# Output projection and router of a transformer block: elementwise work from GpSimd to VectorE, the second norm's variance by ScalarE, two weight loads on another queue

## The chip, the core and the metric

The kernel runs on one core of one Trainium2 chip. A core has five engines that work side by side, each through its own instructions in order: TensorE (PE, matrix products and transposes), VectorE (DVE), ScalarE (ACT), GpSimd (POOL) and SyncE (SP, which here only issues DMA transfers). They meet through semaphores: an instruction that needs another engine's result waits, and everything behind it on its own engine waits too. The metric is device time in microseconds (us) for one execution; less is better.

## What is computed

The reference is one layer of a diffusion transformer on 1024 tokens of width 1024: two kinds of attention, an output projection, two layer norms, and a mixture of 16 experts in which each expert picks its 128 best tokens. The part that the change touches is this:

```python
mix = (sigmoid(g_mla) * (y_mla @ w_proj_mla) + sigmoid(g_na) * (y_na @ w_proj_na)) @ w_out
x_new = layer_norm(ALPHA * x + g1 * mix, ln1_g, ln1_b)
u2 = layer_norm(x_new) * (1 + sc2) + sh2
aff = softmax(u2 @ w_router)              # 16 experts
g, idx = top_k(aff.T, 128)                # each expert's tokens
xe = u2[idx]                              # gathered, then the experts' FFN
```

All of it is float32. The big products split each operand into a high and a low part (hi, lo) and run three products for one.

## The kernel before

The order of instructions on each engine is the order in which the Python code is written; no scheduler moves anything. After attention (which ends near 951 us of the profiled span) three stages follow, then the experts (from about 1213 us to the end).

**Mix stage**, 951 to 1056 us. `split(hi, lo, src, eng)` (L85) makes the two parts: ScalarE copies the high part, then `eng` subtracts it from the source to give the low part. The attention output `yT` is split in 16 pieces of 128x512; a list `POOL` gives five of these to GpSimd. A loop over `m` (8 blocks of 128 output columns) and `b` (two halves of the tokens) then runs 24 products each, and `gates()` (L1150 and following) on VectorE multiplies them by the stored sigmoid gates (`t`, L1153) and adds the two halves into `mix` (L1156). In each `m` SP loads the gates (`sg`, L1080), a block of `w_out` (`wos`, L1131) and the next block of projection weights (`raw`, L1007); the next gate load waits for a buffer that `gates()` frees. `wos_load` multiplies the `w_out` block by `g1b` on GpSimd (L1132). Eight blocks of 128x1024 of `wos` are then split for the output projection (`wo_split`), two of them (`WOP`) with their low part on GpSimd.

**Output and router stage**, 1056 to 1180 us: eight products `main(t, ps, between)`, one for each 128 tokens, each of two halves (b = 0, 1) of 24 matmuls (L1233). The dictionary `between` hangs other work in front of a given matmul group (b, kt). During product t the following runs:
- at its start `pre_mix(t + 1)` splits the next product's input: ScalarE's copy, then the low part on GpSimd (L87, 128x1024);
- `half(t, 0)` and, at the end, `half(t, 1)`: residual and statistics (L1243, L1244) on VectorE;
- `norms(t)` after it: first layer norm on VectorE, with the power -0.5 on GpSimd (L99, `lr`), then the statistics of the second norm (L1264, L1248), its own power on GpSimd, and `nm`, a 128x1 product (L1273);
- for the tokens of t - 1: `route` (transposes L1293 on PE, copied out by ScalarE as `uT`, L1294), `norms2` (L1280 on ScalarE, then L1281 and L1282 on GpSimd, 128x1024 each), `logits` (PE L1301, copied out as `part`), `softmax` (a PE product `collect` L1308, then L1321 to L1331 on VectorE with an Exp on ScalarE);
- `store(t - 2)`: two DMA issues on ScalarE's queue (L1253, L1254).

**Router's end**, 1180 to 1205 us: for expert 0 the rank of each token is counted by comparisons (`compare`, masks on VectorE and GpSimd; `count` on PE), `pick` (L1454) finds its tokens, and `fetch` (L1461) gathers their rows of u2 by an indirect DMA on GpSimd's queue. The first expert's products wait for this transfer.

**Expert weights** come in 1 MB tiles through a ring of 17 buffers (`slot_of_ring`, `load_next`, L1213), in the order in which the experts use them. The ring takes over the buffers of the stages before as these fall free: tiles 13 and 14 use the last `wo` pair.

Of the kernel before, what the change touches and what calls it, by code (L numbers as in the profile page):

```python
# [27 lines left out]
def block_kernel(ctx, tc, a, out, dbg=None):  # L28

    nc = tc.nc  # L30
# [971 lines left out]
    with ExitStack() as st:  # L1002
# [11 lines left out]
        nxt = [(hi, lo)]  # L1014
        POOL = ((0, 3), (1, 5), (1, 7), (1, 1), (1, 3))
# [98 lines left out]
        def pre_mix(t, pieces=1):  # L1114
# [4 lines left out]
            def piece(i):  # L1119
                ks = slice(i * w, (i + 1) * w)  # L1120
                split(hi[:, ks], lo[:, ks], m[:, ks], nc.gpsimd if t else nc.vector)
            return [lambda i=i: piece(i) for i in range(pieces)]

        def wo_split(b, g):
            hi, lo = wo[b, g] = big_tile(), big_tile()
            for k in range(0, 4, 2):
                split(hi[:, k:k + 2], lo[:, k:k + 2], wos[:, 4 * g + k:4 * g + k + 2, b * 512:(b + 1) * 512],
                      nc.gpsimd if (b, 2 * g + k // 2) in WOP else nc.vector)
# [5 lines left out]
        WOP = ((1, 0), (1, 3))  # L1134
        wos_load(0)
# [80 lines left out]
    with ExitStack() as st:  # L1216
# [18 lines left out]

        sts, mv2, u2s, nms = {}, {}, {}, {}

# [18 lines left out]
        def norms(t):  # L1256
            xt = xts[t]
            mv, r = aggregate(sts.pop(t))
            nc.vector.scalar_tensor_tensor(xt, xt, mv[:, 0:1], l1g, op0=OP.subtract, op1=OP.mult)
            for c in (H0, H1):  # L1260
                nc.vector.scalar_tensor_tensor(xt[:, c], xt[:, c], r[:, 0:1], l1b[:, c], op0=OP.mult, op1=OP.add)
            st = p.tile([128, 2, 6], F32, name="st2", bufs=2)
            for b, c in enumerate((H0, H1)):
                nc.vector.bn_stats(st[:, b], xt[:, c])  # L1264
            if t == 7:
                compare(5, 7, 0, 6, nc.gpsimd)
            mv, r = mv2[t] = aggregate(st)
            u2s[t] = p.tile([128, D], F32, name="u2", bufs=2)
            if t == 7:
                nc.vector.scalar_tensor_tensor(u2s[t][:, H1], xt[:, H1], mv[:, 0:1], sc2b[:, H1], op0=OP.subtract, op1=OP.mult)  # L1270
                nc.vector.scalar_tensor_tensor(u2s[t][:, H1], u2s[t][:, H1], r[:, 0:1], sh2b[:, H1], op0=OP.mult, op1=OP.add)
            nms[t] = p.tile([128, 1], F32, name="nm", bufs=2)
            nc.vector.scalar_tensor_tensor(nms[t], mv[:, 0:1], -1.0, r[:, 0:1], op0=OP.mult, op1=OP.mult)  # L1273

        def norms2(t):

            c = H0 if t == 7 else slice(0, D)
            u2, (mv, r) = u2s[t], mv2[t]
            nm = nms.pop(t)
# [107 lines left out]
        for t in range(8):  # L1387
# [9 lines left out]
            else:  # L1397
                between[0, 7] = lambda: route(t - 1, 0)
                between[1, 0] = lambda: route(t - 1, 1)
                between[1, 2] = lambda: (norms2(t - 1), logits(t - 1))  # L1400
                between[1, 4] = lambda: softmax(t - 1)
            if t >= 2:
                between[0, 3] = lambda: store(t - 2, nc.scalar)
            if t == 7:
# [3 lines left out]
                between[0, 1] = lambda: spread(0, 6)  # L1408
                between[0, 5] = between[0, 6] = load_next
                between[1, 3] = lambda: [compare(j, 6) for j in range(3)]  # L1410
# [12 lines left out]
        store(6, nc.scalar)  # L1423
        logits(7)
        compare(5, 7, 6, 7, nc.gpsimd)
        compare(6, 7, 0, 7, nc.gpsimd)
        collect(7)
        compare(3, 6)
        count(rank, 3)
        softmax0(7)  # L1430
        for _ in range(3):
            load_next()
        norms2(7)
        store(7, nc.sync)
        compare(4, 7)
        count(rank, 4)
        softmax1(7)
        spread(7, 8)
# [26 lines left out]
        fetch(xe0, idx0)  # L1465
        while pos[0] < RB - 2:
            load_next(nc.gpsimd)
        pt = ps_T()
# [458 lines left out]
```

## Time and profile before

| | us |
|---|---|
| median of 3 runs (lowest, highest) | 1846.52 (1845.69, 1850.57) |
| the profiled execution | 1849.55 |
| its span, first to last instruction | 1847.8 |
| busy in the span: PE, DVE, ACT, POOL | 1693.6, 1202.8, 939.4, 688.2 |
| eight products and router's end, 1056 to 1205 us | 149 |

The profile gives for each engine when it was busy and, for an idle stretch, whose signal ended it. A busy engine is not always at work: an instruction that is held up after its start counts as busy. Start times are us from the span's start. A row of the timeline merges like instructions (xN) and shows, in brackets, the idle time before it and what ended this.

### The profile page before, as it was taken

To read this page: it belongs to the slowest core of one execution; us is meant where nothing else is said; L and a number is where in the kernel's file an instruction comes from. 1 tells how busy PE (TensorE), PEld (TensorE's weight loads), DVE (VectorE), ACT (ScalarE), POOL (GpSimd) and SP (SyncE) were. 2 spreads that over 40 slices of the span, in tenths; PEclk is the share of its full clock that TensorE was granted. 3 is DMA by queue.
4 is the path that set the end of the run, shared out by engine and by line. 5 is a ranking of instruction groups with operands and counts; after the bars stand their busy time and mean duration, and the time that the engine had idled before them with its cause. 6 is when DMAs were issued, how large, how long until landed. Compare 5 with 4: busy or idle time off the path is not lost.

```text
span 1847.8 us, 25506 instructions
## 1 busy us (share of the span) xinstructions
PE 1693.6 (92%) x9633; PEld 1344.2 (73%) x9633; DVE 1202.8 (65%) x1849; ACT 939.4 (51%) x1479; POOL 688.2 (37%) x528
## 2 busy tenths in 40 slices
PE   5999998999899999999999888778999999999992
PEld 3778787888778877777767666446887887888872
DVE  5612242203477766655563588877999999999987
ACT  3422222111467766666650222244777777777765
POOL 1335455532244421221022355555434423533134
PEclk9999999999999999999999999879999999999996
DMA  8333645245344220110026443687999999999943
GB/s 319 110 108 146 227 167 176 94 118 158 82 87 87 54 54 20 28 30 2 1 88 202 151 182 143 233 314 267 347 396 369 391 391 366 388 391 379 374 158 124
DMA packets 96891, 356.63 MB, mean 193 GB/s; under 512 B 28368, under 2 KB 36944, under 8 KB 70912
## 3 DMA queue, kind: packets, MB, share of 16 engines
q1 hardware_dynamic: 77744, 283.68, 42.4%
q0 software_dynamic: 11664, 43.52, 7.7%
q10 hardware_dynamic: 7360, 27.81, 3.9%
q8 instruction: 75, 1.23, 0.3%
q14 instruction: 48, 0.39, 0.1%
HBM read 312.85 MB, written 42.12 MB: 192 GB/s over the span
## 4 chain that ended last, share of the span: by engine, by line
PE 66%; DVE 12%; DMA 7%; POOL 7%; issue 3%; ACT 3%; SPq 1%; ACTq 0%; POOLq 0%; DVEq 0%
PE pS L401 10%; PE pY L921 4%; DMA rawm<-in_w_mod_dram 4%; PE pT L894 4%; PE pgate L90 3%; PE pD L90 3%; PE pD L92 3%; PE pD L91 3%; PE pup L90 3%; PE pup L91 3%; PE pup L92 3%; PE pgate L92 3%; PE pgate L91 3%; DMA raw<-in_w_proj_dram 2%; PE pS L90 2%
## 5 line engine op out<-in xcount | busy, mean ns | idle before, releaser
L1690 DVE TENSOR_TENSOR hl<-raw,hl 128x1024 fp32r<-128x1024 f32 x183 | 221.7, 1238 | 23.0 <-ACT hl L1689 21.0
L1689 ACT ACTIVATE hl<-raw 128x1024 fp32r<-128x1024 f32 x188 | 194.0, 1056 | 40.4 <-PE pgate L92 19.4
L87 DVE TENSOR_TENSOR wlo<-raw,whi 128x1024 fp32r<-128x1024 f32 x25 | 37.6, 1508 | 148.6 <-ACT whi L86 148.5
L1589 POOL TENSOR_SCALAR oh<-iot,slot 128x128 bf16<-128x128 f32 x112 | 133.2, 1204 | 0.5
L401 PE MATMUL pS<-uhi,whi 128*128 128x512 f32 (+1 forms) x440 | 131.0, 386 | 2.3 <-DVE stg L488 1.5
L401 PE MATMUL pS<-ulo,whi 128*128 128x512 f32 (+1 forms) x440 | 129.0, 382 | 0.0
L401 PE MATMUL pS<-uhi,wlo 128*128 128x512 f32 (+1 forms) x440 | 128.6, 381 | 0.0
L306 POOL TENSOR_TENSOR sb<-qs,sa 128x512 fp32r<-128x512 f32 x28 | 35.9, 1283 | 240.5 <-DVE sa L305 110.0
L1793 POOL DMA_INDIRECT acc_d<-ye,idx x15 | 35.3, 2351 | 242.2 <-DVE ye L1788 242.2
L1689 ACT ACTIVATE whl<-raw 128x1024 fp32r<-128x1024 f32 x94 | 99.7, 1060 | 43.7 <-PE pgate L92 20.0
L1690 DVE TENSOR_TENSOR whl<-raw,whl 128x1024 fp32r<-128x1024 f32 x91 | 112.1, 1232 | 9.4 <-ACT whl L1689 8.5
L905 ACT ACTIVATE pt<-pT 128x512 f32<-128x512 f32 x128 | 69.7, 595 | 95.2 <-PE pT L894 95.0
L1690 DVE TENSOR_TENSOR raw<-raw 128x1024 fp32r<-128x1024 f32 x92 | 112.4, 1222 | 6.6 <-ACT raw L1689 6.6
L1689 ACT ACTIVATE raw<-raw 128x1024 fp32r<-128x1024 f32 x94 | 99.4, 1058 | 22.8 <-PE pD L92 8.2
L376 POOL TENSOR_TENSOR rawm<-rawm,scol 128x1024 f32<-128x1024 f32 x32 | 63.1, 1971 | 127.3 <-DMA rawm<-in_w_mod_dram 127.3
L880 DVE TENSOR_REDUCE sn<-pS 128x1 f32<-128x1024 f32 x64 | 78.3, 1223 | 40.5 <-PE pS L92 40.3
L1233 PE MATMUL pS<-raw,hl 128*128 128x512 f32 x384 | 97.8, 403 | 3.3 <-DVE t L1153 2.2
L401 PEld LDWEIGHTS pS<-uhi,whi 128*128 128x128 f32 x440 | 78.9, 188 | 22.9 <-issue 3.9
L894 PE MATMUL pT<-ident,pm 128*128 128x128 f32 x640 | 94.5, 278 | 1.2 <-ACT pt L905 1.0
L401 PEld LDWEIGHTS pS<-ulo,whi 128*128 128x128 f32 x440 | 80.2, 188 | 16.4
L921 PE MATMUL pY<-pt,v 128*64 128x256 f32 x640 | 82.5, 389 | 10.5 <-ACT inv L721 10.5
L401 PEld LDWEIGHTS pS<-uhi,wlo 128*128 128x128 f32 x440 | 80.1, 188 | 16.3
(482 smaller groups left out, 4773.4 us busy)
## 6 DMA issues: line engine op xcount, KB each, us to landing
raw<-in_w_exp_down_dram SPq DMA_DIRECT2D x64, 1024.0 KB
raw<-in_w_exp_gate_dram SPq DMA_DIRECT2D x63, 1024.0 KB
raw<-in_w_exp_up_dram SPq DMA_DIRECT2D x63, 1024.0 KB
rawm<-in_w_mod_dram POOLq DMA_DIRECT2D x32, 512.0 KB, 3.8
raw<-in_w_in_dram SPq DMA_DIRECT2D x25, 512.0 KB
wm<-in_w_mod_dram SPq DMA_DIRECT2D x8, 1024.0 KB
sig_d<-stg ACTq DMA_DIRECT2D x16, 512.0 KB
sg<-sig_d SPq DMA_DIRECT2D x32, 256.0 KB
```

The costliest lines, as they stand in the source:

```text
L90: nc.tensor.matmul(ps, ahi, bhi, start=first, stop=False)
L91: nc.tensor.matmul(ps, ahi, blo, start=False, stop=False)
L92: nc.tensor.matmul(ps, alo, bhi, start=False, stop=last)
L401: nc.tensor.matmul(pt[:, c0:c1], ww[:, kt], uu[:, kt, c0:c1], start=(kt == 0 and k == 0), stop=(kt == KT - 1 and k == 2))
L880: nc.vector.tensor_reduce(sm[:, 0:1], ps, axis=AX.X, op=OP.max)
L894: nc.tensor.transpose(tb[b][:, (k - k0) * 128:(k - k0 + 1) * 128], Pm[n][:, k * 128:(k + 1) * 128], ident)
L905: nc.scalar.activation(dst, src, AF.Copy)
L921: nc.tensor.matmul(py[0][h * 64:(h + 1) * 64, 0:256], vm[:, k, col:col + 64], PT[g, h][:, k], start=(k == 0), stop=(k == 9))
L1233: nc.tensor.matmul(ps[b], x[:, kt], w[:, kt % 4], start=(kt == 0 and k == 0), stop=(kt == 7 and k == 2))
L1589: nc.gpsimd.tensor_scalar(ohb[:, t], iot, slot[:, t, e:e + 1], None, op0=OP.is_equal)
L1689: nc.scalar.activation(w[:, 0], src, AF.Copy)
L1690: lo_on(e, i).tensor_tensor(w[:, 1], src, w[:, 0].bitcast(F32), op=OP.subtract)
```

## The change

1. Every `split` in these stages makes its low part on VectorE, and so does the multiplication of `wos` by `g1b`: five pieces of 128x512, two of 128x1024 of `wo`, one of 128x1024 in each `pre_mix(t)` from t = 1, and eight multiplications of 128x1024 leave GpSimd.
2. For t < 7 the two halves of the first norm's last step also sum their output (`accum_out`); a 128x1 step makes the mean, ScalarE squares the deviations (one 128x1024 `Square` with a sum), and `deviation` makes the factor 1/sigma in the next product. The second `bn_stats` pass, its aggregation and `nm` go.
3. `norms2` becomes two 128x1024 steps on VectorE behind `softmax`; the ScalarE step and both GpSimd steps go. For t = 7 all of it is on VectorE, and the order behind the last product is another.
4. Five ring loads stand on SP right behind the last product; before, three of them stood further down on SP and two on GpSimd's queue behind `fetch`.

```diff
-                    split(yhl[s, b][0][:, k], yhl[s, b][1][:, k], yT[:, c, cols], nc.gpsimd if (b, c) in POOL else nc.vector)
+                    split(yhl[s, b][0][:, k], yhl[s, b][1][:, k], yT[:, c, cols])
...
-                split(hi[:, ks], lo[:, ks], m[:, ks], nc.gpsimd if t else nc.vector)
+                split(hi[:, ks], lo[:, ks], m[:, ks])
...
-            nc.gpsimd.tensor_tensor(wos[:, m], wos[:, m], g1b, op=OP.mult)
+            nc.vector.tensor_tensor(wos[:, m], wos[:, m], g1b, op=OP.mult)
...
+            sm = p.tile([128, 4], F32, name="sums", bufs=3)
+            for b, c in enumerate((H0, H1)):
+                nc.vector.scalar_tensor_tensor(xt[:, c], xt[:, c], r[:, 0:1], l1b[:, c], op0=OP.mult, op1=OP.add,
+                                               accum_out=sm[:, b:b + 1])
+            nc.vector.tensor_scalar(sm[:, 2:3], sm[:, 0:1], sm[:, 1:2], 1.0 / D, op0=OP.add, op1=OP.mult)
+            nc.scalar.activation(u2s[t], xt, AF.Square, scale=-1.0, bias=sm[:, 2:3], accum_out=sm[:, 3:4])
...
+        def deviation(t):
+            mean, _ = mv2[t]
+            v = p.tile([128, 1], F32, name="v2", bufs=2)
+            nc.vector.tensor_scalar(v, spread2[t], 1.0 / D, 1e-5, op0=OP.mult, op1=OP.add)
+            r = p.tile([128, 1], F32, name="r2", bufs=3)
+            nc.gpsimd.tensor_tensor(r, v, mhalf[:, 0:1], op=OP.pow)
...
-            nc.scalar.activation(u2[:, c], xts[t][:, c], AF.Identity, scale=r[:, 0:1], bias=nm)
-            nc.gpsimd.tensor_tensor(u2[:, c], u2[:, c], sc2b[:, c], op=OP.mult)
-            nc.gpsimd.tensor_tensor(u2[:, c], u2[:, c], sh2b[:, c], op=OP.add)
+                nc.vector.scalar_tensor_tensor(u2s[t], xts[t], mv[:, 0:1], sc2b, op0=OP.subtract, op1=OP.mult)
+                nc.vector.scalar_tensor_tensor(u2s[t], u2s[t], r[:, 0:1], sh2b, op0=OP.mult, op1=OP.add)
...
-                between[1, 2] = lambda: (norms2(t - 1), logits(t - 1))
-                between[1, 4] = lambda: softmax(t - 1)
+                between[0, 4] = lambda: deviation(t - 1)
+                between[1, 2] = lambda: logits(t - 1)
+                between[1, 4] = lambda: (softmax(t - 1), norms2(t - 1))
...
             main(t, ps, between)
+            if t == 7:
+                while pos[0] < RB - 2:
+                    load_next()
...
-        while pos[0] < RB - 2:
-            load_next(nc.gpsimd)
```

ScalarE in one product (tokens of the product before: `uT`, `part`, `ex`; `hl` is the split for the next product; the two DMA rows are the store). Before:

```order
L1294 ACTIVATE uT<-pT 128x512 x2
L1280 ACTIVATE u_9622<-xt,nm,lr 128x1024
L1304 ACTIVATE part<-pY 128x128
L1325 ACTIVATE ex,sm<-lt,sm 128x16
L86 ACTIVATE hl<-raw 128x1024
L1253 DMA u_d<-u_9622 128x1024
L1254 DMA acc_d<-xt 128x1024
```

And after the change, from the same place on:

```order
L1302 ACTIVATE uT<-pT 128x512 x2
L1312 ACTIVATE part<-pY 128x128
L1333 ACTIVATE ex,sm<-lt,sm 128x16
L1272 ACTIVATE u_9722,sums<-xt,sums 128x1024
L86 ACTIVATE hl<-raw 128x1024
L1250 DMA u_d<-u_9606 128x1024
L1251 DMA acc_d<-xt 128x1024
```

The 128x1024 step on `u` has left its place between `uT` and `part` and stands, as the Square, at the end of the product, ahead of the split `hl`, the store and the next product's `uT`.

VectorE in one product, from the end of the first norm to the next half of a product. Before:

```order
L1261 SCALAR_TENSOR_TENSOR xt<-xt,lr,l1b 128x512 x2
L1264 BN_STATS st_9613<-xt 128x6 x2
L1248 BN_AGGR mv<-st_9613 128x2
L97 TENSOR_SCALAR lv<-mv 128x1
L1273 SCALAR_TENSOR_TENSOR nm<-mv,lr 128x1
L1243 SCALAR_TENSOR_TENSOR xt<-xt,pS 128x512
L1244 BN_STATS st<-xt 128x6
L1321 SCALAR_TENSOR_TENSOR lt<-cb,mv,pY 128x16
L1322 SCALAR_TENSOR_TENSOR lt<-lt,lr,cb 128x16
L1323 TENSOR_REDUCE sm<-lt 128x1
L1330 RECIPROCAL sm<-sm 128x1
L1331 TENSOR_SCALAR vals<-ex,sm 128x16
```

And after the change (the rows from L1329 to L1338 are those of L1321 to L1330, left out here):

```order
L1269 SCALAR_TENSOR_TENSOR xt,sums<-xt,lr,l1b 128x512 x2
L1271 TENSOR_SCALAR sums<-sums 128x1
L87 TENSOR_TENSOR hl<-raw,hl 128x1024
L1279 TENSOR_SCALAR v_9633<-sums 128x1
L1240 SCALAR_TENSOR_TENSOR xt<-xt,pS 128x512
L1241 BN_STATS st<-xt 128x6
...
L1339 TENSOR_SCALAR vals<-ex,sm 128x16
L1288 SCALAR_TENSOR_TENSOR u_9606<-xt,sums,sc2b 128x1024
L1290 SCALAR_TENSOR_TENSOR u_9606<-u_9606,r_9635,sh2b 128x1024
L1240 SCALAR_TENSOR_TENSOR xt<-xt,pS 128x512
```

The statistics pass has gone; the low part `hl` and the two 128x1024 steps on `u` have come, the latter ahead of `half(t, 1)`.

VectorE in the mix stage, from the `gates()` of one `m` to those of the next (`raw` in the second kind of row is `mix`, `hl` the low part of the next projection weights). Before:

```order
L1153 TENSOR_TENSOR t<-pS,sg 128x1024
L1156 TENSOR_TENSOR raw<-t 128x256 x2
L87 TENSOR_TENSOR hl<-raw,hl 128x1024
L1153 TENSOR_TENSOR t<-pS,sg 128x1024
L1156 TENSOR_TENSOR raw<-t 128x256 x2
```

And after the change:

```order
L1150 TENSOR_TENSOR t<-pS,sg 128x1024
L1153 TENSOR_TENSOR raw<-t 128x256 x2
L1130 TENSOR_TENSOR wos<-wos,g1b 128x1024
L87 TENSOR_TENSOR hl<-raw,hl 128x1024
L1150 TENSOR_TENSOR t<-pS,sg 128x1024
L1153 TENSOR_TENSOR raw<-t 128x256 x2
```

The multiplication of `wos`, which waits for its own DMA, now stands ahead of the weights' split and of `gates()`.

## Rows read from the trace of the kernel before

**Rows 1.** Busy time of the engines in two stretches: start:end, length, then by engine.

```profile
1118.90:1134.60 15.70, 13.25 (x75) 10.15 (x74) 13.15 (x20) 4.07 (x7) 9.18 (x6) 1.00 0.28 102
1400.00:1500.00 100.00, 100.00 (x475) 80.20 (x474) 94.36 (x100) 77.31 (x85) 34.18 (x26) 1.00 1.00 382
```

**Rows 2.** TensorE's timeline in the products: start, duration, line, shapes, count, [idle before].

```profile
1131.83 7.73 PE L1233 MATMUL pS<-raw,hl 128*128 128x512 f32 x33
1143.71 0.64 PE L1301 MATMUL pY<-uT,wr 128*32 128x128 f32 x16
1147.32 0.40 PE L1308 MATMUL pY<-esel,part 128*128 128x16 f32 x2 [1.38 <-ACT part L1304]
```

**Rows 3.** Single lines of softmax: count, minimum, median and maximum duration in ns.

```profile
L1322 DVE SCALAR_TENSOR_TENSOR lt<-lt,lr,cb x8: 235/1576/1587, 1085.0 to 1196.3; 128x16 f32<-128x16 f32 x8
L1331 DVE TENSOR_SCALAR vals<-ex,sm x8: 234/1609/1622, 1087.5 to 1197.9; 128x16 f32<-128x16 f32 x8
```

**Rows 4.** VectorE's timeline in the products, columns as in TensorE's.

```profile
1089.03 0.67 DVE L1243 SCALAR_TENSOR_TENSOR xt<-xt,pS 128x512 f32<-128x512 f32 x1
1143.50 2.33 DVE L1273 SCALAR_TENSOR_TENSOR nm<-mv,lr 128x1 f32<-128x1 f32 x1 [0.73 <-POOL lr L99]
1152.00 0.68 DVE L1243 SCALAR_TENSOR_TENSOR xt<-xt,pS 128x512 f32<-128x512 f32 x1
1153.75 1.28 DVE L1259 SCALAR_TENSOR_TENSOR xt<-xt,mv,ye 128x1024 f32<-128x1024 f32 x1
1155.47 1.41 DVE L1261 SCALAR_TENSOR_TENSOR xt<-xt,lr,l1b 128x512 f32<-128x512 f32 x2 [0.44 <-POOL lr L99]
```

**Rows 5.** GpSimd's timeline beside it.

```profile
1143.43 2.38 POOL L87 TENSOR_TENSOR hl<-raw,hl 128x1024 fp32r<-128x1024 f32 x1
```

**Rows 6.** ScalarE's timeline: a copy and a store behind the last product, a Square.

```profile
1191.94 0.60 ACT L1294 ACTIVATE uT<-pT 128x512 f32<-128x512 f32 x1 [0.20 <-PE pT L1293]
1192.00 0.33 ACTq L1253 DMA_DIRECT2D u_d<-u  x1
1811.50 1.15 ACT L1816 ACTIVATE xe<-raw,er 128x1024 f32<-128x1024 f32 x1
```

**Rows 7.** VectorE's timeline at the start of the mix stage.

```profile
952.49 2.49 DVE L87 TENSOR_TENSOR raw<-yT,raw 128x512 fp32r<-128x512 f32 x4
962.20 3.15 DVE L87 TENSOR_TENSOR raw<-yT,raw 128x512 fp32r<-128x512 f32 x2
966.55 1.23 DVE L1153 TENSOR_TENSOR t<-pS,sg 128x1024 f32<-128x1024 f32 x1 [1.19 <-POOL raw L87]
```

**Rows 8.** Low parts of `wos` by tile (ns), and TensorE at the first product.

```profile
L87 DVE TENSOR_TENSOR raw<-wos,raw x6: 1212/1218/3237, 1056.2 to 1069.1; 128x1024 fp32r<-128x1024 f32 x6
1065.41 4.65 PE L1233 MATMUL pS<-raw,hl 128*128 128x512 f32 x13 [2.23 <-DVE t L1153]
```

**Rows 9.** Eighth product and router's end: VectorE, GpSimd, TensorE.

```profile
1176.60 2.69 DVE L1360 TENSOR_SCALAR mask<-hl,vals 128x640 bf16<-128x640 f32 x1
1179.22 2.45 DVE L1362 SCALAR_TENSOR_TENSOR tie<-hl,vals,ut 128x128 bf16<-128x128 f32 x1
1184.94 0.68 DVE L1243 SCALAR_TENSOR_TENSOR xt<-xt,pS 128x512 f32<-128x512 f32 x1
1196.70 0.55 DVE L1358 TENSOR_SCALAR hl<-hl,vals 128x640 bf16<-128x640 f32 x1
1205.43 1.10 POOL L1461 DMA_INDIRECT xe<-u_d,idx  x1 [3.52 <-DVE uT L1454]
1212.90 1.08 PE L1624 MATMUL pY<-ident,xe 128*128 128x128 f32 x4 [8.13 <-DMA xe<-u_d,idx]
```

**Rows 10.** VectorE reads a sum out after `pick`.

```profile
1203.80 0.08 DVE L1454 DVE_READ_ACCUMULATOR uT<-pS,col,hl 128x1 f32 x1
```

**Rows 11.** One `m` of the mix stage: GpSimd on `wos`, ScalarE on the weights.

```profile
1040.07 2.40 POOL L1132 TENSOR_TENSOR wos<-wos,g1b 128x1024 f32<-128x1024 f32 x1 [8.41 <-DMA wos<-in_w_out_dram]
1041.53 1.06 ACT L86 ACTIVATE hl<-raw 128x1024 fp32r<-128x1024 f32 x1 [10.90 <-DMA raw<-in_w_proj_dram]
```

More of the change, by code (lines that the diff above doesn't have):

```diff
@@ L1014, in block_kernel @@
         nxt = [(hi, lo)]
-        POOL = ((0, 3), (1, 5), (1, 7), (1, 1), (1, 3))
         yhl = {}
@@ L1126, in wo_split @@
             for k in range(0, 4, 2):
-                split(hi[:, k:k + 2], lo[:, k:k + 2], wos[:, 4 * g + k:4 * g + k + 2, b * 512:(b + 1) * 512],
-                      nc.gpsimd if (b, 2 * g + k // 2) in WOP else nc.vector)
+                split(hi[:, k:k + 2], lo[:, k:k + 2], wos[:, 4 * g + k:4 * g + k + 2, b * 512:(b + 1) * 512])
         def wos_load(m):
             nc.sync.dma_start(wos[:, m], a["w_out"][m * 128:(m + 1) * 128])
-            nc.gpsimd.tensor_tensor(wos[:, m], wos[:, m], g1b, op=OP.mult)
-        WOP = ((1, 0), (1, 3))
+            nc.vector.tensor_tensor(wos[:, m], wos[:, m], g1b, op=OP.mult)
         wos_load(0)
@@ L1234, in main @@
                                          start=(kt == 0 and k == 0), stop=(kt == 7 and k == 2))
-        sts, mv2, u2s, nms = {}, {}, {}, {}
+        sts, mv2, spread2, u2s = {}, {}, {}, {}
         def half(t, ps, b):
@@ L1259, in norms @@
             nc.vector.scalar_tensor_tensor(xt, xt, mv[:, 0:1], l1g, op0=OP.subtract, op1=OP.mult)
[L1260 to L1267, printed above, removed]
@@ L1268, in norms @@
             u2s[t] = p.tile([128, D], F32, name="u2", bufs=2)
             if t == 7:
[L1270 to L1279, printed above, removed]
-            nc.scalar.activation(u2[:, c], xts[t][:, c], AF.Identity, scale=r[:, 0:1], bias=nm)
-            nc.gpsimd.tensor_tensor(u2[:, c], u2[:, c], sc2b[:, c], op=OP.mult)
-            nc.gpsimd.tensor_tensor(u2[:, c], u2[:, c], sh2b[:, c], op=OP.add)
+                st = p.tile([128, 2, 6], F32, name="st2", bufs=1)
+                for b, c in enumerate((H0, H1)):
+                    nc.vector.scalar_tensor_tensor(xt[:, c], xt[:, c], r[:, 0:1], l1b[:, c], op0=OP.mult, op1=OP.add)
@@ new lines, in norms @@
+                for b, c in enumerate((H0, H1)):
+                    nc.vector.bn_stats(st[:, b], xt[:, c])
+                mv2[t] = aggregate(st)
+                compare(5, 7, 0, 6, nc.gpsimd)
+                return
+            sm = p.tile([128, 4], F32, name="sums", bufs=3)
+            for b, c in enumerate((H0, H1)):
+                nc.vector.scalar_tensor_tensor(xt[:, c], xt[:, c], r[:, 0:1], l1b[:, c], op0=OP.mult, op1=OP.add,
+                                               accum_out=sm[:, b:b + 1])
@@ new lines, in norms @@
+            nc.vector.tensor_scalar(sm[:, 2:3], sm[:, 0:1], sm[:, 1:2], 1.0 / D, op0=OP.add, op1=OP.mult)
+            nc.scalar.activation(u2s[t], xt, AF.Square, scale=-1.0, bias=sm[:, 2:3], accum_out=sm[:, 3:4])
+            mv2[t], spread2[t] = (sm[:, 2:3], None), sm[:, 3:4]
+        def deviation(t):
[4 more added lines that the diff above has]
+            nc.gpsimd.tensor_tensor(r, v, mhalf[:, 0:1], op=OP.pow)
+            mv2[t] = mean, r
@@ L1284, in block_kernel, with norms2 @@
+        def norms2(t, only=None):
+            mv, r = mv2[t]
+            if only != 1:
+                nc.vector.scalar_tensor_tensor(u2s[t], xts[t], mv[:, 0:1], sc2b, op0=OP.subtract, op1=OP.mult)
+            if only != 0:
+                nc.vector.scalar_tensor_tensor(u2s[t], u2s[t], r[:, 0:1], sh2b, op0=OP.mult, op1=OP.add)
         uts, lg = {}, {}
@@ L1409, in block_kernel @@
                 between[0, 5] = between[0, 6] = load_next
+                between[1, 4] = lambda: softmax(t - 1)
+                between[1, 5] = lambda: norms2(t - 1)
                 between[1, 3] = lambda: [compare(j, 6) for j in range(3)]
@@ L1424, in block_kernel @@
         logits(7)
+        norms2(7, 0)
         compare(5, 7, 6, 7, nc.gpsimd)
@@ L1427, in block_kernel @@
         collect(7)
+        softmax0(7)
+        norms2(7, 1)
+        store(7, nc.sync)
+        softmax1(7)
         compare(3, 6)
         count(rank, 3)
[L1430 to L1434, printed above, removed]
         compare(4, 7)
         count(rank, 4)
-        softmax1(7)
         spread(7, 8)
```

## The prediction

> **What bounds the kernel now.** I read the views in this order: busy time by stretch, the timelines of TensorE and VectorE inside one product, the lines whose duration has a median far above its minimum, and GpSimd's timeline beside these.
>
> The stretches show two regimes [rows 1]. Between 1400 and 1500 us TensorE is busy for all 100 us: the experts are bound by it, and it waits for no weight load there. In a product of the output and router stage neither TensorE (13.25 of 15.70) nor VectorE (13.15) is full, so there the time is set by a chain across engines. The reader should see that a second saved before the experts is a second saved at the end: the first expert's transposes wait 8.13 us for the gather, which is issued at 1205.43 behind the last `pick` [rows 9], and the experts behind it run at TensorE's pace.
>
> The chain through one product runs from one `half(t, 1)` to the next. It starts at 1089.03 and, four products later, at 1152.00 [rows 4]: 62.97 / 4 = 15.74 us each. TensorE's rows name the wait: `collect` stands idle for 1.38 us until ScalarE's `part` is there [rows 2]. `part` is late because the 128x1024 `u` step stands ahead of it on ScalarE, and that step needs `nm`. On VectorE three small steps are far longer than their work [rows 3, 4]: `nm` takes 2.33 us, L1322 1.58 where its minimum is 0.235, L1331 1.61 where its minimum is 0.234. The end of `nm` (1143.50 + 2.33 = 1145.83) is the end of GpSimd's low part (1143.43 + 2.38 = 1145.81) [rows 5]. So VectorE is held while GpSimd runs a 128x1024 step. Taking 0.23 for a small step that is not held, the holds come to 2.1 + 1.35 + 1.38 = 4.8 of VectorE's 13.15 us in a product.
>
> **The change part by part.**
>
> *Mix stage.* VectorE starts the last run of low parts at 962.20; two of them take 3.15, held beside GpSimd, and `gates()` then waits 1.19 more for GpSimd's own last one, until 966.55 [rows 7]. After the change four stand there, at 2.49 / 4 = 0.62 each, 2.5 in all; then the multiplication of `wos`, about 1.2 as any 128x1024 two-operand step (1.218 [rows 8]): 962.20 + 2.5 + 1.2 = 965.9. `gates()` free the buffer for the next gate load, and the weights queue behind that load, so the whole stage moves: -0.7; bounds 0 (the weights' own transfer sets the pace) and -0.95. The other seven multiplications now stand on VectorE ahead of the weights' low part. In the tightest `m`, `wos` lands at 1040.07 and the weights at 1041.53 [rows 11], a lead of 1.46 for a step of 1.2, while ScalarE's high part of the weights (1.06) runs first in any case. VectorE has been idle there, so I cost them at nothing; without that cover a rival below has the price.
>
> *First product.* VectorE makes six low parts of `wos` at 1.22, but one takes 3.24, held beside GpSimd's two [rows 8]. TensorE waits 2.23 for the last `gates()`, which is queued behind them. After the change there are eight on VectorE, two of them behind the `gates()`. The hold goes, 2.0, but one more low part stands ahead: -0.8 for the `gates()`. I take -1.0, since the steps behind the `gates()` are no longer held either. Bounds: 0, and -2.8 (the whole wait goes, and TensorE does not run 0.36 a matmul behind it, 4.65 / 13, but 0.234, 7.73 / 33 [rows 2]).
>
> *The six full intervals.* The new chain, step by step:
> - from `half(t, 1)` to the end of the second half of x: 1155.47 + 1.41 - 1152.00 = 4.88 [rows 4]. The sum has to be read out: 0.08, from the nearest row, a VectorE step with a sum [rows 10]; then the 128x1 mean, 0.15 (less than the 0.235 of a 128x16 step). Together 5.1.
> - ScalarE: the Square, 1.15, with its sum read out, 0.2 (an estimate, twice VectorE's); the high part, 1.06 [rows 11]; two `uT`, 0.60 each [rows 6]: 3.6, less some 0.25 in which consecutive rows overlap: 3.35. The store's two issues stand here too. They cost nothing as long as ScalarE's queue issues them while the step ahead still executes: the issue at 1192.00 began 0.06 after the `uT` of 1191.94 had begun [rows 6].
> - TensorE: `logits` 0.64, six matmuls at 0.234, 1.4, `collect` 0.40 [rows 2]: 2.45. `part` is no longer behind the `u` step, so the 1.38 goes.
> - `softmax`: `collect` ends at 1147.72 and the next half starts at 1152.00, 4.28 [rows 2, 4]. The holds in it go, 1.35 + 1.38 = 2.72 [rows 3]: 1.56.
> - `norms2`, now ahead of the half: two 128x1024 steps at 1.28 [rows 4], 2.5.
>
> Sum: 5.1 + 3.35 + 2.45 + 1.56 + 2.5 = 14.95, against 15.74: -0.79, times six -4.7. No engine is late next: TensorE's own work is 13.25. VectorE's is at most 13.15 - 4.8 + 1.22 (low part) + 2.5 + 0.4 = 12.5, with no credit for the statistics that go. GpSimd keeps small powers alone.
>
> *Eighth product and router's end.* `half(7, 1)` now starts at 1184.94, 17.2 after the one before (1152.00 + 15.74 = 1167.7). Two comparisons in between are held: 2.69 for 128x640 and 2.45 for 128x128 [rows 9]; a 128x640 one alone takes 0.55, so at least 2.1 + 1.9 = 4.0 goes. `norms2` adds 2.5. VectorE starts `half(7, 0)` some 0.7 earlier, as `nm` and the second statistics are gone. So -4.0 + 2.5 - 0.7 = -2.2. Behind it the second norm of the last tokens leaves GpSimd and ScalarE, other holds go, and a longer step on `u` comes: -0.7, an estimate. Together -2.9; bounds -1 (the `norms2` steps add fully and the comparisons were waiting anyway) and -5.5 (the gather, 7.4 from issue to use, also gets faster by up to 2, since no ring loads are issued right behind it).
>
> *Ring loads.* Three of the five are issued where they were in time, the other two some 25 us earlier. They are tiles of the second expert, needed after the gather. Cost 0; bounds 0 and the -2 above. `store(7)` is queued behind them on SP, but its rows of `u2` are made 15 us later.
>
> Total: -0.7 - 1.0 - 4.7 - 2.9 = -9.3. The profiled execution took 1849.55, of which the span is 1847.8, and lies 3.0 above the median of 1846.52; the difference is taken from the median: **1837.2**.
>
> **The rivals.**
>
> *The store is not covered.* If ScalarE's issues run after the high part and not beside it, 0.33 and 0.45 lie on the chain: 15.7, no gain in the intervals, and a total of -4.6, 1841.9. For it: on the chain ScalarE is at work without a gap, and the one overlap in the rows is with a `uT`. Against it: that row.
>
> *A sum on VectorE is not cheap.* The rows of L1454 show 0.08 for reading the sum, but there one of the two big operands is in the matmul accumulator; both of L1269 are float32 in SBUF. If such a step ran at half its rate, the two halves would take 1.34 each, not 0.70, and the interval 16.25: +0.5 times six, and a total of -4.6 + 3.1 = -1.5, 1845.0. The rows hold nothing nearer. The Trainium skill states this rule ("Vector Engine (DVE) Microarchitecture Reference", Points that are easy to get wrong): this kind of step with two sources in SBUF that are not bf16 runs at half throughput, since no read port is left for the accumulator. The row without a sum (two in 1.41, so 0.7 each for 512 columns) shows no halving of the plain step, and no row here shows it with a sum.
>
> *`wos` lands behind the weights (slower).* VectorE works in order: if in an `m` the transfer of `wos` comes later than the weights', the weights' low part, the products and the gate load all wait for it. The point is a lead under some 0.15 (1.2 of work less the 1.06 of ScalarE's high part); the lead is 1.46 in the tightest `m` [rows 11]. Were the order of the two landings turned round by the same 1.46 to 2.9, six of the blocks would wait about 2.9 each, +17.5, and the time would be 1854.7. Against it: both loads are on one queue, `wos` first.
>
> *The change does not do what it says*: some hold stays, because GpSimd still runs a power while VectorE works. It takes half of the 4.0 to 4.8 back and ends near the first rival; I count it there.
>
> **How the numbers follow.** Forecast 0.72; store or holds 0.14; sum at half rate 0.08; `wos` late 0.06. What a measurement of this kernel can tell from no change is about 0.3%, 5.5 us. The forecast's own bounds, with the terms' ends not all at once, are 1831 to 1841; so faster 0.72. The two middle rivals lie within 0.3%: same 0.22. Slower 0.06. For 8 in 10 the range takes in the first rival and the near ends of the second: 1831 to 1844.
>
> **What the profile of after would show.** `gates()` of the first `m` at 965.9. `wos` multiplied before the weights' low part begins in every `m`. `half(t, 1)` every 14.95 us; L1269 at 0.7 each, not 1.34; the store's issue beginning inside the high part; L1330 and L1339 at 0.23; `logits`, not `collect`, waiting for ScalarE. `half(7, 1)` some 9 us earlier than now, and 7.4 us or less from gather to transposes. An interval of 15.7 or more, or VectorE waiting for `wos` while weights are there, would make the prediction wrong.

## The result

The changed kernel takes 1834.2 us, median of four runs (1833.15 to 1836.0), against 1847.64 for the kernel before, timed beside it: a ratio of 0.992 (95% interval 0.9909 to 0.9932). Timed again on another occasion it was 1831.55 against 1849.7, 0.9903 (0.9887 to 0.992). The forecast was faster by 9.3 us, to 1837.2; it became faster by 13.4. That is inside the stated 1831 to 1844, though near its lower end (1831.55 the second time).

Where the profiled executions differ, by marks that both timelines have. The start of the first mark itself moved by +1.10 us between these two executions, and lies anywhere in 7.6 us (943.31 to 950.95) among profiles that are alike up to there; so every stage is measured from the mark ahead of it.

| stage, from mark to mark, us | before | after | difference | forecast |
|---|---|---|---|---|
| last reciprocal of attention to the first `gates()` | 16.70 | 15.48 | -1.22 | -0.7 |
| to `gates(7, 0)`, the last but one | 84.35 | 87.97 | +3.62 | 0 |
| to `half(0, 1)`, the end of the first product | 22.27 | 17.27 | -5.00 | -1.0 |
| to `half(6, 1)`, six intervals | 94.55 | 88.20 | -6.35 | -4.7 |
| to `half(7, 1)` | 17.22 | 14.76 | -2.46 | -2.2 |
| to the issue of the first gather | 20.49 | 20.01 | -0.48 | -0.7 |
| to the first expert's transposes | 7.47 | 5.21 | -2.26 | 0 |
| sum | 263.05 | 248.90 | -14.15 | -9.3 |

With the +1.10 ahead of them that is -13.05; the spans differ by 13.6. Behind the first transposes little changed, as forecast.

**One product after the change.** VectorE's timeline from one `half(t, 1)` to the next (start, duration, line, shapes, [idle before and who ended it]), the answer to [rows 4]:

```profile
1115.81 0.68 DVE L1240 SCALAR_TENSOR_TENSOR xe<-xe,pS 128x512 f32<-128x512 f32 x1
...
1119.96 0.75 DVE L1269 SCALAR_TENSOR_TENSOR xe<-xe,lr,l1b 128x512 f32<-128x512 f32 x1
1120.64 0.08 DVE L1269 DVE_READ_ACCUMULATOR xe<-xe,lr,l1b 128x1 f32 x1
1120.76 0.21 DVE L1271 TENSOR_SCALAR sums<-sums 128x1 f32<-128x1 f32 x1
1123.23 1.22 DVE L87 TENSOR_TENSOR hl<-raw,hl 128x1024 fp32r<-128x1024 f32 x1 [2.26 <-ACT hl L86]
...
1126.74 0.24 DVE L1330 SCALAR_TENSOR_TENSOR lt<-lt,r,cb 128x16 f32<-128x16 f32 x1
...
1127.84 0.24 DVE L1339 TENSOR_SCALAR vals<-ex,sm 128x16 f32<-128x16 f32 x1
...
1129.30 1.28 DVE L1290 SCALAR_TENSOR_TENSOR u<-u,r,sh2b 128x1024 f32<-128x1024 f32 x1
1130.50 0.68 DVE L1240 SCALAR_TENSOR_TENSOR xt<-xt,pS 128x512 f32<-128x512 f32 x1
```

The interval is 1130.50 - 1115.81 = 14.69 us, against 15.74. L1330 and L1339 take 0.24 each where L1322 and L1331 took 1.58 and 1.61 [rows 3]. The step with a sum takes 0.75 and its read-out 0.08. The two steps of `norms2` stand right ahead of the next half, 2.5 us. ScalarE beside it, the answer to [rows 6]:

```profile
1121.01 1.15 ACT L1272 ACTIVATE u<-xe,sums 128x1024 f32<-128x1024 f32 x1 [8.08 <-DVE sums L1271]
1121.01 0.33 ACTq L1250 DMA_DIRECT2D u_d<-u  x1
...
1122.15 1.04 ACT L86 ACTIVATE hl<-raw 128x1024 fp32r<-128x1024 f32 x1
1123.11 1.06 ACT L1302 ACTIVATE uT<-pT 128x512 f32<-128x512 f32 x2
```

The store's issue begins with the Square and is over inside it and the high part: it costs nothing on the chain. TensorE, the answer to [rows 2]:

```profile
1123.73 0.92 PE L1309 MATMUL pY<-uT,wr 128*32 128x128 f32 x16 [0.38 <-ACT uT L1302]
...
1126.07 0.29 PE L1316 MATMUL pY<-esel,part 128*128 128x16 f32 x2
```

`logits` waits 0.38 for `uT`, and `collect` waits for nothing. One interval by busy time (columns as in [rows 1]):

```profile
1115.81:1130.50 14.69, 13.33 (x76) 10.17 (x75) 10.58 (x22) 3.84 (x8) 2.01 (x2) 1.00 0.31 110
```

VectorE is busy for 10.58 us, not 13.15. TensorE's own 13.33 is the least that an interval can take with this work.

**The mix stage and the first product.** VectorE's timeline (the multiplication of `wos` is L1130, `gates()` L1150, the low parts of `wos` L87), the answer to [rows 7, 8, 11]:

```profile
1040.06 1.23 DVE L1130 TENSOR_TENSOR wos<-wos,g1b 128x1024 f32<-128x1024 f32 x1 [3.12 <-DMA wos<-in_w_out_dram]
...
1053.26 1.23 DVE L1130 TENSOR_TENSOR wos<-wos,g1b 128x1024 f32<-128x1024 f32 x1 [4.39 <-DMA wos<-in_w_out_dram]
1054.40 1.22 DVE L1150 TENSOR_TENSOR t<-pS,sg 128x1024 f32<-128x1024 f32 x1
...
1057.73 6.90 DVE L87 TENSOR_TENSOR raw<-wos,raw 128x1024 fp32r<-128x1024 f32 x6
1064.55 1.22 DVE L1150 TENSOR_TENSOR t<-pS,sg 128x1024 f32<-128x1024 f32 x1
```

The multiplication at 1040.06 ends before ScalarE even has the weights (its high part starts at 1042.69), as forecast. In the last block there are no weights, and there the multiplication stands straight ahead of `gates(7, 0)`: VectorE waits 4.39 us for `wos`. TensorE's timeline behind it, and the granted clock (the last but two columns of the second row: 1.00; it was 0.83 there before):

```profile
1065.91 10.49 PE L1230 MATMUL pS<-raw,hl 128*128 128x512 f32 x45 [1.11 <-DVE t L1150]
...
1065.00:1075.00 10.00, 9.09 (x40) 7.56 (x41) 9.16 (x13) 0.36 (x2) 1.31 (x1) 1.00 0.46 163
```

**The gather** (GpSimd's issue, then TensorE's first transposes), the answer to [rows 9]:

```profile
1194.64 1.09 POOL L1474 DMA_INDIRECT xe<-u_d,idx  x1 [6.26 <-DVE idx L1469]
...
1199.85 1.08 PE L1635 MATMUL pY<-ident,xe 128*128 128x128 f32 x4 [5.70 <-DMA xe<-u_d,idx]
```

### The profile page after: what moved, and what is told of

It is laid out like the page before. It is cut to its first block, busy times and chain, and to the rows that moved or that the text cites. A ratio compares the mean times of both kernels' runs of the same rounds, so it can differ in the third digit from the quotient of the medians.

```text
span 1834.2 us, 25492 instructions
## 1 busy us (share of the span) xinstructions
PE 1689.9 (92%) x9633; PEld 1342.5 (73%) x9633; DVE 1184.6 (65%) x1877; ACT 937.0 (51%) x1485; POOL 595.7 (32%) x488
## 5 line engine op out<-in xcount | busy, mean ns | idle before, releaser
L87 DVE TENSOR_TENSOR wlo<-raw,whi 128x1024 fp32r<-128x1024 f32 x25 | 36.9, 1478 | 152.0 <-ACT whi L86 152.0
```

## The experiments

Nearly all of what follows is read from the traces by the marks of the table above, since medians of the same code scatter by two or three us (1834.2 and 1831.55 for the change). From the first mark to the end of the span the profiles take 897.9 us in the kernel before, 898.2 with the fourth part alone, 880.7 with the first and fourth, 883.3 and 882.5 with the whole change, 881.8 to 884.6 in the five variants of it that leave `norms2` in place, and 873.3 to 874.5 in the three that move it.

**The ring loads: the fourth part undone, then alone.** First the change without it:

```diff
-            if t == 7:
-                while pos[0] < RB - 2:
-                    load_next()
...
+        for _ in range(3):
+            load_next()
         softmax1(7)
...
         fetch(xe0, idx0)
+        while pos[0] < RB - 2:
+            load_next(nc.gpsimd)
```

> The change with its fourth part undone: three ring loads further down on SP, two on GpSimd's queue behind the gather. Theory (the 2.26 us that the gather gained, 7.47 to 5.21 from issue to the first transposes, come from the two ring loads no longer being issued right behind it): gather to transposes back at about 7.4 us, median 2 us above the change's, some 1836. Rival (the gather gained by something else, such as u2 stored earlier): 5.2 us stays and the time is the change's.

Measured: 1833.15 us, ratio to before 0.9924 (0.9898 to 0.995). GpSimd's, TensorE's and VectorE's timelines:

```profile
1187.54 1.09 POOL L1473 DMA_INDIRECT xe<-u_d,idx  x1 [5.86 <-DVE idx L1468]
...
1188.62 8.15 DVE L1468 TENSOR_TENSOR gg<-picked 128x1 f32<-128x1 f32 x1
...
1197.44 1.09 PE L1636 MATMUL pY<-ident,xe 128*128 128x128 f32 x4 [10.76 <-DVE top L1518]
```

From issue to transposes it is 9.90 us, more than the theory said, but the time is not above the change's. The theory got the wait and not what it is worth: the 128x1 addition for `gg`, a step of VectorE that took 0.16 in the kernel before, took 8.15 beside GpSimd here. The search for the other experts' tokens is queued behind it and was late as well. From the gather to the second expert's sums on TensorE it took 65.46 us, as in four other profiles with such a hold and a gather of under 5 us (64.96 to 65.53); so the longer gather cost nothing there. Then the kernel before with this part alone:

> The kernel before with the fourth part alone, the five ring loads behind the last product. Theory (the gather is slowed by the store of the last tokens, which here is still issued only 3 us ahead of it, as in the run with the first and fourth part, where it took 7.41): gather to transposes 7.2 to 7.6 us, time that of the kernel before within 2 us. Rival (the two ring loads behind the gather slow it): 4.7 to 5.3 us, time 2 to 3 us below.

Measured: 1848.9 us, ratio 0.9999 (0.9987 to 1.0012). The gather's issue and the transposes:

```profile
1205.11 1.09 POOL L1462 DMA_INDIRECT xe<-u_d,idx  x1 [3.48 <-DVE uT L1455]
...
1213.24 1.09 PE L1623 MATMUL pY<-ident,xe 128*128 128x128 f32 x4 [9.53 <-DMA xe<-u_d,idx]
```

8.13 us, a little over the theory's range and far from the rival's. So the fourth part alone brings nothing, and moving the two loads off GpSimd is not by itself what made the gather faster. In the three profiles in which the store was issued 3.5 us ahead of the gather (the kernel before, this one, and one below) the latter took 7.41 to 8.13; in the nine in which it was issued 8.7 to 9.5 us ahead, and no load stood on GpSimd's queue, 4.64 to 5.21.

That fits the theory's number, but not its cause. In the three, the store's last packet ended 0.1 us behind the gather's issue, and the gather's first packet came only 1.8 us behind it (3.6 in this run). What ran beside the gather were the next expert loads on SP's queue. These are the transfers from 1.5 to 3.4 us behind the issue (queue, packets, MB, share of the DMA engines' time; q0 is the gather, q1 SP's loads), first in this run, then in the change:

```profile
q1 hardware_dynamic: 60, 0.49, 84.5%
...
q0 software_dynamic: 83, 0.34, 81.7%
```

In each of the two no other data queue moved anything; in the kernel before and in the run below both did (31 packets of the gather beside 25 of SP's, and 39 beside 32). SP's packets began 1.6 to 2.1 us behind the gather's issue in the three, and 3.5 to 3.6 us in the nine, whose gather was through at 4.2 to 4.7. In the run with 9.90 us above, SP's loads moved data the whole time. So what the gather costs goes with the loads beside it. The third part, which finishes the last `u2` earlier, fits as the reason that they come later: in the nine the gather is issued 0.3 us behind its index, in the three 0.64 to 0.84. That step is argued, since the delay alone was not varied.

**Two low parts back on GpSimd.**

```diff
-                split(hi[:, k:k + 2], lo[:, k:k + 2], wos[...])
+                split(hi[:, k:k + 2], lo[:, k:k + 2], wos[...],
+                      nc.gpsimd if (b, 2 * g + k // 2) in WOP else nc.vector)
```

> The change with the two low parts of wo that GpSimd made before (WOP) given back to it. Theory (TensorE's wait for the last gates() of the mix stage grows back to over 2 us, and its clock then falls as before): a low part on VectorE held to about 3.2 us, TensorE's wait 2 us or more, granted clock below 1 in the 10 us behind it and matmuls at 0.36 us, the first product 2 to 4 us longer. Rival (no clock in it, only the hold): matmuls stay at 0.233, the product is at most 1 us longer.

Measured: 1831.43 us, ratio 0.9909 (0.9883 to 0.9936), so the median does not tell it from the change; the stage does. VectorE, TensorE, and the clock behind the wait:

```profile
1053.46 7.97 DVE L87 TENSOR_TENSOR raw<-wos,raw 128x1024 fp32r<-128x1024 f32 x5
...
1062.71 12.10 PE L1233 MATMUL pS<-raw,hl 128*128 128x512 f32 x45 [1.90 <-DVE t L1153]
...
1064.00:1074.00 10.00, 10.00 (x40) 8.08 (x40) 7.18 (x11) 0.00 (x0) 1.49 (x1) 0.87 0.72 269
```

From `gates(7, 0)` to `half(0, 1)` it took 19.95 us, 2.7 more than the change's 17.27. Of this 1.1 is the later `gates(7, 1)` and 1.6 lies behind it: 45 matmuls in 12.10, 0.27 each, where the change's 45 ran in 10.49, 0.233 each. TensorE had waited 1.90 before, 1.11 in the change, and the granted clock is 0.87, not 1.00. The theory holds in the main: the product is 2.7 us longer and the clock falls, with a wait just under its 2 us and 0.27 instead of 0.36 a matmul. But the wait alone does not settle the clock: in the run with the fourth part alone it was 2.19 at the same place, and the clock stayed at 1.00 (rows in the next section).

**The last `wos` block multiplied later.**

```diff
-            nc.vector.tensor_tensor(wos[:, m], wos[:, m], g1b, op=OP.mult)
+            if m < 7:
+                nc.vector.tensor_tensor(wos[:, m], wos[:, m], g1b, op=OP.mult)
...
                         piece()
+                    nc.vector.tensor_tensor(wos[:, 7], wos[:, 7], g1b, op=OP.mult)
                     wo_split(0, 0)
```

> The change with one instruction moved: the last multiplication of wos by g1b stands behind the low part of the first product's input and not ahead of the last but one gates(). Theory (these gates() waited 2.3 us for the transfer of the last wos block, which nobody needs yet): the wait of 4.4 us for that transfer goes, the first product begins 1.6 to 2.4 us earlier and the time falls by as much, to about 1832. Rival (the first product's splits on ScalarE need that block soon anyway): the wait appears ahead of them and the time is the change's.

Measured: 1834.45 us, ratio 0.993 (0.9904 to 0.9957). VectorE:

```profile
1047.66 1.22 DVE L1151 TENSOR_TENSOR t<-pS,sg 128x1024 f32<-128x1024 f32 x1 [3.42 <-PE pS L92]
...
1050.81 1.22 DVE L1162 TENSOR_TENSOR wos<-wos,g1b 128x1024 f32<-128x1024 f32 x1
...
1058.75 1.21 DVE L1151 TENSOR_TENSOR t<-pS,sg 128x1024 f32<-128x1024 f32 x1
```

`gates(7, 0)` no longer waits for a transfer, but from it to `gates(7, 1)` takes 11.09 us and not 10.15. `half(0, 1)` comes 119.55 us after the first mark; in seven variants that left the multiplication where it was, 118.86 to 119.77, but for the two low parts above, and 118.45 and 120.72 in the change's own two profiles. The rival's outcome came, though not its wait: VectorE is not idle ahead of the multiplication, but its 1.22 us now stand between the two `gates()`. So moving it bought nothing that shows beside this scatter of some 2 us.

**`norms2` behind the next first norm.**

```diff
-                between[1, 4] = lambda: (softmax(t - 1), norms2(t - 1))
+                between[1, 4] = lambda: softmax(t - 1)
...
-                between[0, 3] = lambda: store(t - 2, nc.scalar)
+                between[1, 3] = lambda: store(t - 2, nc.scalar)
...
-                between[1, 3] = lambda: [compare(j, 6) for j in range(3)]
+                between[1, 3] = lambda: (store(t - 2, nc.scalar), [compare(j, 6) for j in range(3)])
...
             norms(t)
+            if 0 < t < 7:
+                norms2(t - 1)
```

> The change with the two 128x1024 steps of norms2 moved behind the next first norm, where VectorE sits idle for 2.26 us before the low part, and the store moved to the last third of the product. Theory (norms2's 2.5 us stand on the chain ahead of the second half of each product, which is in PSUM about 1.2 us before): intervals 13.5 instead of 14.69 us, six of them 7 us, the time about 1827. Rival (VectorE's own work then delays the low part and the logits, or the store delays ScalarE): intervals 14.2 or more.

Measured: 1825.51 us, ratio 0.988 (0.9852 to 0.9908). VectorE:

```profile
1093.72 0.69 DVE L1240 SCALAR_TENSOR_TENSOR xt<-xt,pS 128x512 f32<-128x512 f32 x1 [1.18 <-PE pS L1230]
...
1098.81 1.27 DVE L1288 SCALAR_TENSOR_TENSOR u<-xt,sums,sc2b 128x1024 f32<-128x1024 f32 x1
...
1107.16 0.69 DVE L1240 SCALAR_TENSOR_TENSOR xe<-xe,pS 128x512 f32<-128x512 f32 x1 [1.17 <-PE pS L1230]
```

The interval is 13.44, as the theory said; the half now waits 1.17 for TensorE's product, so this chain is no longer the bound. The eighth product gave back 1.07 us (15.83 from `half(6, 1)` to `half(7, 1)`, not 14.76), because one more `norms2` stands in it.

**The first and fourth part alone** (norms as in the kernel before):

> The kernel before with the first and fourth part of the change alone: all low parts and the multiplication of wos on VectorE, the ring loads behind the last product; norms2 as before, one step on ScalarE and two on GpSimd. Theory (of the 4.8 us in which VectorE is held per product, the 2.1 of nm come from the low part on GpSimd, and they delay the u step, part and collect; the other two holds stay but move with them): nm at 0.15, L1322 and L1331 still up to 1.6, collect no longer waiting 1.38, interval 13.6 to 14.2 us, so that this part alone brings as much as the whole change or more. Rival (all holds have to go to gain): interval 15 us or more.

Measured: 1830.15 us, ratio 0.9891 (0.9869 to 0.9913). VectorE and TensorE in one product:

```profile
1108.80 0.68 DVE L1242 SCALAR_TENSOR_TENSOR xe<-xe,pS 128x512 f32<-128x512 f32 x1
...
1116.04 0.16 DVE L1272 SCALAR_TENSOR_TENSOR nm<-mv,lr 128x1 f32<-128x1 f32 x1 [0.73 <-POOL lr L99]
...
1118.91 1.08 DVE L1321 SCALAR_TENSOR_TENSOR lt<-lt,lr,cb 128x16 f32<-128x16 f32 x1
...
1120.86 1.60 DVE L1330 TENSOR_SCALAR vals<-ex,sm 128x16 f32<-128x16 f32 x1
1122.38 0.67 DVE L1242 SCALAR_TENSOR_TENSOR xt<-xt,pS 128x512 f32<-128x512 f32 x1
...
1118.31 0.29 PE L1307 MATMUL pY<-esel,part 128*128 128x16 f32 x2
```

The theory holds. `nm` takes 0.16, the two softmax steps are still held (1.08 and 1.60), yet the interval is 1122.38 - 1108.80 = 13.58 us, shorter than the change's, since `collect` waits for nothing and no `norms2` stands ahead of the half. The end is as before: 17.20 to `half(7, 1)`, 20.46 to the gather, 7.41 from there. From the first mark to the end of the span it takes 880.7 us, against 883.3 and 882.5 in the change: the first part, with the fourth, brings at least what the whole change brings.

**One low part back on GpSimd**, the one of each next product's input:

```diff
-                split(hi[:, ks], lo[:, ks], m[:, ks])
+                split(hi[:, ks], lo[:, ks], m[:, ks], nc.gpsimd if t else nc.vector)
```

> The change with one step given back to GpSimd: the low part of each next product's input, 128x1024. Theory (what counts is which VectorE step meets it: here it runs from some 0.1 to 2.5 us after ScalarE's high part ends, where VectorE has only the half of the product and its statistics): interval 14.7 to 15.3 us. Rival (every 128x1024 step on GpSimd holds VectorE on the chain for its 2.4 us): interval 16.5 to 17 us.

Measured: 1832.57 us, ratio 0.9906 (0.9886 to 0.9927). GpSimd, and VectorE beside it:

```profile
1106.82 0.68 DVE L1240 SCALAR_TENSOR_TENSOR xe<-xe,pS 128x512 f32<-128x512 f32 x1
...
1114.28 2.38 POOL L87 TENSOR_TENSOR hl<-raw,hl 128x1024 fp32r<-128x1024 f32 x1 [4.02 <-ACT hl L86]
...
1113.40 0.69 DVE L1240 SCALAR_TENSOR_TENSOR xt<-xt,pS 128x512 f32<-128x512 f32 x1
1117.42 0.23 DVE L1329 SCALAR_TENSOR_TENSOR lt<-cb,sums,pY 128x16 f32<-128x16 f32 x1 [2.60 <-PE pY L1316]
```

While the low part runs (1114.28 to 1116.66) VectorE has only statistics to do and then nothing. The interval to this half is 1121.51 - 1106.82 = 14.69, to the hundredth that of the change (six take 88.35, not 88.20). The theory holds at its lower end: in the change's order this move is worth nothing.

**The weights of expert 0 by a reduction.**

```diff
-        pick(gg0, brow, 2)
+        for b, c in enumerate((H0, H1)):
+            nc.vector.scalar_tensor_tensor(junk[:, c], rank[b], col, brow[:, c], ..., accum_out=picked[:, 2 + b:3 + b])
+        nc.vector.tensor_reduce(gg0, picked[:, 2:4], axis=AX.X, op=OP.add)
```

> The change with one 128x1 step written in another form: the sum of the two halves of gg (expert 0's weights) by a reduction of one operand, not by an addition of two. In three variants of the change that addition took 7.0 to 8.2 us, held beside three low parts on GpSimd, with the 16 rounds of the top-k search queued behind it; in the change's own profile it began 0.09 us before the first of them and took 0.16. Theory (a step with one operand is not held): 0.1 to 0.3 us in any run, gather to the second expert's sums 63.5 to 64.5 us, never 65 and more; time 0 to 1 us below the change's. Rival (held all the same): 7 us in the profile in some runs, no gain.

Measured: 1832.98 us, ratio 0.9902 (0.988 to 0.9924).

```profile
1192.53 0.15 DVE L1488 TENSOR_REDUCE gg<-picked 128x1 f32<-128x2 f32 x1
```

The step takes 0.15, and from the gather to the second expert's sums it is 64.05 us, in the theory's range. With two more profiles of this form, below, it was held in none of three (63.28, 63.50, 64.05), but only the one here tests the form. The addition was held in five of seven profiles of the change and its variants: 64.96 to 65.53 where it was, 63.48 and 64.43 where it was not. In the five, GpSimd's next work began 0.01 to 0.04 us behind the addition's start, in the two 0.09 and 0.36. Behind the reduction it began 0.03 us later in this run, but 0.59 and 0.82 in the two below, where an addition would hardly have been held either. So the hold is real and costs some 1.3 us (from the gather to the end of the span 640.9 to 641.6 where it was held, 638.4 to 639.6 in the other five); that a step with one operand cannot be held is likely but rests on one profile, and the medians (1832.98 against 1834.2 and 1831.55) are too coarse for it.

**Both of the moves that were thought to gain.**

> norms2 behind the next first norm and the store later (as in the run that measured 1825.5) together with the reduction for gg. Theory: the two are independent; intervals 13.5 us, the step of gg 0.1 to 0.3 us, time 1824 to 1826, 8 to 10 us below the change. Rival (a part hides the other): 1826 or more.

Measured: 1824.44 us, ratio 0.9865 (0.9845 to 0.9886). To compare it with the change on one chip, both were timed again, the change first:

> The change itself, beside the next two. Theory: 0.991 to 0.993 of the kernel before; intervals 14.69 us as in its first profile, whatever attention ahead of it takes in this run.

> The variant with norms2 behind the next first norm and the reduction for gg, on the same chip as the change. Theory: intervals 13.5 against 14.69 us, six of them 7 us, less 1.1 us given back in the eighth product: 6 to 9 us below the change, 0.995 to 0.997 of its time. Rival (no more than the scatter between runs): within 3 us of the change.

Measured: 1831.55 us (ratio 0.9903, 0.9887 to 0.992) and 1825.64 us (0.9872, 0.9856 to 0.9889). The intervals are 14.70 and 13.45, six of them 88.22 and 80.68 us.

The second lies 5.9 us below the change, just short of the 6 to 9 expected: 7.5 less in the six intervals, 1.1 more in the eighth product, and what lies around scatters by a microsecond or two. This version beats both kernels, and nearly all of it is the place of `norms2`.

## Why the prediction was right, and where not

- **What bounds the stage** was read rightly. A chain across engines set the products and VectorE was held beside GpSimd; with GpSimd's large steps gone every small step is short, and the time saved passed on to the end.
- **The mix stage**: the first `gates()` came 1.22 us earlier (forecast 0.7), in every variant with the first part, at 15.48 after the first mark. Some 0.4 of it was gained ahead of the row at 962.20 from which the forecast started, where the weights' low part took 2.32 beside GpSimd and takes 1.21 now. By `gates(6, 1)` about half of it is left: 95.96 and 96.10 us after the first mark in two profiles with the old order, 94.3 to 95.9 in eleven with the new one. What the forecast did not have is the last block, in which `wos` is multiplied ahead of `gates(7, 0)`. It waits there for its transfer, and `gates(7, 0)` comes 7.54 us after `gates(6, 1)`, not 5.09. This is the place that the rival on `wos` described, at the one block for which it was not worked out. The run with the later multiplication gained nothing by avoiding it, within the scatter of some 2 us.
- **The first product** is the term that was mis-sized: -1.0 forecast, -5.0 measured (-2.6 together with the two stages ahead of it, and -3.5 to -4.9 in the other profiles with the first part, the one with the two low parts back aside). The low parts ahead of `gates(7, 1)` gave 1.1, near the 0.8 worked out for them (five took 7.98, six take 6.90). What was not counted is the hold on the two small additions behind `gates(7, 0)`: 2.78 us beside the multiplication of `wos` on GpSimd, 0.76 now. And the hold on those behind `gates(7, 1)`, for which the forecast had 0.2, was worth 2.0: they took 3.86 beside GpSimd's low parts and take 0.76, and the low part that TensorE needs next stands behind them. From `gates(7, 1)` to `half(0, 1)` it was 9.11 and is 7.12. VectorE, TensorE and the clock in the kernel before:

```profile
1052.16 2.78 DVE L1156 TENSOR_TENSOR raw<-t 128x256 f32<-128x256 f32 x2
...
1065.30 3.86 DVE L1156 TENSOR_TENSOR raw<-t 128x256 f32<-128x256 f32 x2
...
1070.35 7.54 PE L1233 MATMUL pS<-raw,hl 128*128 128x512 f32 x32 [0.29 <-DVE raw L87]
...
1065.00:1075.00 10.00, 9.30 (x33) 7.07 (x34) 8.28 (x11) 1.06 (x1) 3.88 (x2) 0.83 0.36 104
```

- **The clock**, which the forecast held as the far bound of this term, went from 0.83 to 1.00, but had no share in the gain. The run with the fourth part alone has these stages as in the kernel before, and its clock stayed at 1.00: its first 13 matmuls ran in 3.21 us and not in 4.65, and then TensorE waited 1.75 for that same low part and not 0.29. From `gates(7, 1)` to `half(0, 1)` it took 9.15 us, as the kernel before did. Only where no such wait follows, in the run with two low parts back on GpSimd, did the lower clock cost something (1.6 us).

```profile
1065.12 3.21 PE L1233 MATMUL pS<-raw,hl 128*128 128x512 f32 x13 [2.19 <-DVE t L1153]
1070.08 7.56 PE L1233 MATMUL pS<-raw,hl 128*128 128x512 f32 x32 [1.75 <-DVE raw L87]
...
1065.00:1075.00 10.00, 8.13 (x35) 6.44 (x36) 8.30 (x10) 1.06 (x1) 3.70 (x3) 1.00 0.37 115
```

- **The six intervals**: -6.35 measured, -4.7 forecast. The sum was 14.95 and became 14.69. To the mean 5.16 (5.1); ScalarE 3.20 (3.35); TensorE 2.19 (2.45), since `logits` begins when the first `uT` is there; softmax and `norms2` 4.14 (4.06). The first interval is a little longer than the others in both kernels (15.86 and 14.77), which adds next to nothing. So the sum by steps was right to 2%; the gain, a difference of two large numbers, came out a third larger than forecast.
- **What the sum hid**: the forecast put the gain down to the holds that go, and the second and third part of the change into the same account. The runs tell them apart. The first part alone brings the interval to 13.58; the other parts with the low part left on GpSimd bring 14.69; all together 14.69. So it was enough that `nm` and GpSimd's low part no longer meet, in either manner, and putting `norms2` ahead of the half then cost 1.1 per interval (1.25 by the run that moves it). The sentence "No engine is late next" was right of engines, but the forecast's own list of steps had 2.5 us of `norms2` in the chain that nobody needs there, and did not ask whether they could stand elsewhere. Beside the first and fourth part alone, the second and third lose 6.6 us in the six intervals (88.20 against 81.59) and win 5.1 behind them (next point).
- **Eighth product and router's end**: -2.9 forecast, -2.94 measured. Here the second and third part pay: with the norms of before this stretch takes 2.44 + 0.45 more, and the gather 2.2 more.
- **The gather and the ring loads**: moving the loads was costed at 0, which is right (ratio 0.9999 alone). The 2.26 that the gather gained stood in the bounds of the term before, but under the wrong loads: those on GpSimd's queue, where the ones that it had run beside were SP's next. Not foreseen: GpSimd's next work now begins about when the addition for `gg` does, and where it began within 0.04 us of it the addition was held, which costs some 1.3 us.
- **The rivals**: the store is covered, its issue starting with the Square. The sum costs 0.75 and 0.08, so no half rate: the Trainium skill's rule ("Vector Engine (DVE) Microarchitecture Reference", Points that are easy to get wrong) does not show in this row, with both operands float32 in SBUF. `wos` did not land behind the weights in any `m`.

## What to carry to other kernels

When a small step on one engine takes ten times its minimum, look for the large step on another engine that ends with it, and then ask which of the two is easier to move: here either move ended the hold that mattered, and `norms2`, which the second put into the chain, cost more in the products than the move brought there. After working out a new chain step by step, go through it once more for steps whose result is not needed at its end; the 2.5 us that were listed here without that question were worth 6 us. Compare stages by marks of their own, as medians of the whole kernel could not tell most of these variants apart.

## What was not expected of the hardware

A 128x1 addition of two operands on VectorE took 8.15 us beside GpSimd's work (7.02 or 7.03 in four other runs), while steps such as the reciprocal at 1134.53 in the kernel before (0.16), or the search steps behind that addition in the change's profile (0.67 each), ran at their usual length in the middle of a GpSimd step. In these rows it is the form of a step that decides whether it is held, not its size.

The gather of 128 rows took from 4.6 to 9.9 us from issue to use, with the same rows to fetch: longest with expert loads moving data the whole time, 7.4 to 8.1 where they began 1.6 to 2.1 us behind its issue, and 4.6 to 5.2 where they began 3.5 us behind it.

TensorE's granted clock fell behind waits of 1.90 and 2.23 us in the first product (to 0.87 and 0.83 over the next 10 us, a mean over a stretch at 0.50, the level of 1.2 GHz, and full speed around it), but not behind one of 2.19 at the same place, nor behind one of 1.11. The length of that wait alone does not tell whether it falls, and what does was not found.
